# Moving the displaced column blocks of the weights' low parts in the two feed-forward products of a hybrid decoder layer

## The chip, the cores and the metric

One core of a Trainium2 chip runs the kernel alone. The metric is the device time of one execution in microseconds. The kernel before took 2131.19 us, the median of three runs (2129.93, 2131.19 and 2131.62 us).

## The reference

One decoder layer for 512 tokens of width 2048 in fp32, with a hidden width of 8192 in the feed-forward part:

```python
mod = silu(c) @ W_ada + b_ada            # shift1, scale1, gate1, shift2, scale2, gate2
h   = rms_norm(x) * (1 + scale1) + shift1
u   = h @ W_in
# conv group: B * causal_depthwise_conv3(C * H); attention group: NSA, 8 heads
x   = x + gate1 * (concat(rms_norm(y_conv), rms_norm(y_nsa)) @ W_out)
h   = rms_norm(x) * (1 + scale2) + shift2
x   = x + gate2 * (relu(h @ W1) ** 2 @ W2)
out = rms_norm(x)
```

The last product line is what this document is about: `h @ W1` is the first feed-forward product, the product with `W2` is the second.

## The kernel before, in words

**The products.** Each fp32 operand is split in two: a high part, rounded to the reduced format fp32r, and a low part, the rest. A product is then three matmuls on TensorE: high by high, high by low and low by high (`mm3`, line 347). One matmul takes a block of 128 x 128 weights and 256 columns of tokens (half of the 512). In both feed-forward products pairs of rows and columns of blocks are combined by a seven-product scheme: four blobs of weights of 128 x 1024 (`rw`, 512 KB each, loaded by SP's queue) are added and subtracted on VectorE to give seven operands, called B1, U6, T5, B2, T7, B3 and T4 (`operands`, line 1230).

**The weight tiles.** `hilo` (line 1097) makes the two parts of an operand: ScalarE copies the high part into columns of an `hl` tile, and VectorE subtracts it from the source and writes the low part behind it. There are three `hl` tiles (line 1046), used in turn (`hl_tile`, line 1094). A tile has 2048 + 4 * 16 columns of 4 bytes. An operand has eight blocks of 128 columns, and each is used by three matmuls: the high block twice, then the low block. So one tile serves 24 matmuls, and one turn of the ring of three tiles 72. All these matmuls appear in the profile as `pf<-tk,hl` on line 120, since a helper records every instruction there.

**Displacement.** Where the parts stand within a tile is set by the class `Low` (line 1048) and the lists in `rings` (line 1073):

```python
def __getitem__(self, at):                       # L1053
    a, b = at[1].start, at[1].stop
    o = 1024 + self.places[a // P] * SHIFT       # SHIFT = 16 columns = 64 bytes
    return self.t[:, o + a:o + b]
...
def ring(high, *low):                            # L1069
    return cycle([[t[:, high * SHIFT:high * SHIFT + 1024], Low(t, p)] for t, p in zip(hl, low)])
```

`places[k]` says by how many steps of 64 bytes block `k` of the low part stands to the right of column 1024. In stages 1 and 2 the high part itself starts one step in (`high` is 1), so a low block with place 1 is exactly 1024 columns from its high block, and one with place 2 is displaced by 64 bytes against that. `Low.parts` (line 1058) says in how many VectorE instructions the low part is written: one where all places are equal, one with a pattern of 2 x 512 where the only change is at block 4, and otherwise one for each run of equal places.

**The stages.** Stage 0 is the end of the output projection (`w_oa`). Stage 1 (`stage_of[0] = 1`, line 1138) holds the rest of the output projection (`late_out`, line 1151), 24 parts of the first product for p = 0 to 2 (`part`, line 1347), and 29 rounds of `ff1` (line 1277, p = 3 to 31) of seven operands each, whose results go through relu, a square, a split (`outcome`, line 1260) and DRAM. Stage 2 (line 1442) holds the second product, the loop over f, q, seven operands and two halves j at line 1443, where half j = 0 uses blocks 0 to 3 of an operand and j = 1 blocks 4 to 7; then `plain` (line 1421), the last rows as an ordinary product with the final norm (`finish`, line 1394).

**The order.** The instructions from the output projection on are recorded by the class `Order` and put out at line 1493 in an order that it plans itself by its own costs of instructions. A change in the number of VectorE instructions can so move others, on every engine.

Of the kernel before, what the change touches and what calls it, by code (L numbers as in the profile page):

```python
# [273 lines left out]
def hybrid_layer(ctx: ExitStack, tc: tile.TileContext, a, out):  # L274
# [11 lines left out]
    def slot(dtype=F32, name="m"):  # L286
        return mainp.tile([P, SLOT], dtype, name=name, tag="m")
# [90 lines left out]
    ring = [slot(name="wa")[:, :1024] for _ in range(NWA)]  # L378
# [690 lines left out]
    def ring(high, *low):  # L1069
        return cycle([[t[:, high * SHIFT:high * SHIFT + 1024], Low(t, p)] for t, p in zip(hl, low)])  # L1070

    rings = [ring(0, [0] * 8, [0] * 8, [0] * 8), ring(1, [1] * 8, [1] * 8, [1] * 7 + [2]),
             ring(1, [1] * 8, [1] * 8, [1] * 4 + [2] * 4)]
    stage_of = [0]
    ffp.tile([P, SHIFT], F32, name="shift", bufs=1)
    sg = {t: cycle([ffp.tile([P, 1024], d, name="sg", bufs=2) for _ in range(2)])
# [503 lines left out]
```

## Time and profile before

The profiled execution took 2131.37 us, and the span of its trace is 2129.6 us. It stands 0.18 us above the median.

| what | before |
|---|---|
| median of the runs | 2131.19 us |
| the profiled execution, and its span | 2131.37 us, 2129.6 us |
| TensorE (PE) busy | 2071.7 us, 97%, 15014 matmuls |
| VectorE (DVE) busy | 1889.5 us, 89% |
| ScalarE (ACT) busy | 1008.6 us, 47% |
| matmuls `pf<-tk,hl` | 10704, mean 278 ns |
| bytes moved | 454.17 MB, mean 213 GB/s |

A row of groups gives the line, the engine, the operation, what is written and read (output<-inputs, with buffer numbers left out), the shape, the count, the busy time with the mean of one instruction in ns, and the idle time ahead of them with what ended it. A row of the timeline gives start, length in us, engine, line, operation and how many equal instructions in a row it stands for; a bracket at its end is the wait ahead of it, with its releaser. A matmul's duration overlaps the next one's, so TensorE's pace is the distance from start to start: for a row of N matmuls, its length less the duration of one, divided by N - 1.

### The profile page before, as it was taken

The page shows a single profiled execution, that of the slowest core. Times are in us where ns is not written, and L with a number is a line of the kernel's source. Part 1 is how long each engine was busy: PE and PEld are TensorE (multiplying, and loading weights), DVE is VectorE, ACT ScalarE, POOL GpSimd, SP SyncE. Part 2 cuts the span into 40 slices and gives each one's busy share as a digit, 9 for nine tenths or more (in the row PEclk, how much of TensorE's full clock was granted, in tenths as well). Part 3 has the DMA queues.
Part 4 walks back from the last instruction along what each step waited for, and adds up shares of the span by engine and source line. Part 5 has one row for each costly group of instructions (what it writes and reads, how often), then busy time and mean ns, then how long its engine had stood idle before and what let it go on. Part 6 is the DMA issues. An engine that isn't in the chain of part 4 may idle for free.

```text
span 2129.6 us, 38017 instructions
## 1 busy us (share of the span) xinstructions
PE 2071.7 (97%) x15014; PEld 1930.5 (91%) x15014; DVE 1889.5 (89%) x3045; ACT 1008.6 (47%) x1470; POOL 128.6 (6%) x244
## 2 busy tenths in 40 slices
PE   5999999999999999999999999999999999999997
PEld 3888778898877779999999999999999999999997
DVE  8989888887987656999999999999999999999998
ACT  4532333222454434766666666666433333333345
POOL 0000000000000001021221211111000000000000
PEclk8999999999999999999999999999999999999999
DMA  8995679888321144477766677669876366366452
GB/s 333 346 352 221 217 279 326 308 292 314 108 80 40 50 139 158 129 228 208 221 201 202 199 218 215 202 206 306 309 268 230 128 247 236 130 239 237 136 182 90
DMA packets 144130, 454.17 MB, mean 213 GB/s; under 512 B 15824, under 2 KB 20176, under 8 KB 143952
## 3 DMA queue, kind: packets, MB, share of 16 engines
q1 hardware_dynamic: 108816, 386.72, 52.5%
q0 software_dynamic: 34048, 63.98, 9.5%
q8 instruction: 118, 1.93, 0.4%
q10 hardware_dynamic: 1088, 1.05, 0.1%
q14 instruction: 60, 0.49, 0.1%
HBM read 383.53 MB, written 68.16 MB: 212 GB/s over the span
## 4 chain that ended last, share of the span: by engine, by line
PE 55%; DVE 1%; ACT 1%; issue 0%; DMA 0%; DVEq 0%; ACTq 0%
PE pf L120 55%; DVE x L120 0%; DVE hl L120 0%; ACT t L120 0%; ACT x L120 0%; DMA rw<-in_w_f 0%; DVE rw L120 0%; DVE sg L120 0%; DVE sacc L120 0%; ACT hl L120 0%; DVE t L120 0%; ACT tk L120 0%; DVE gt L120 0%; DVEq L1576 0%; ACT sacc L120 0%
## 5 line engine op out<-in xcount | busy, mean ns | idle before, releaser
L120 PE MATMUL pf<-tk,hl 128*128 128x256 f32 x10704 | 1235.5, 278 | 2.3 <-ACT t L120 1.4
L120 PEld LDWEIGHTS pf<-tk,hl 128*128 128x128 f32 x10704 | 1233.6, 188 | 3.1 <-ACT t L120 1.6
L120 ACT ACTIVATE hl<-rw 128x1024 fp32r<-128x1024 f32 x269 | 285.4, 1062 | 337.5 <-PE pf L120 302.7
L120 DVE TENSOR_TENSOR hl<-rw,hl 128x1024 fp32r<-128x1024 f32 (+2 forms) x314 | 331.9, 1064 | 36.5 <-ACT hl L120 36.5
L120 ACT ACTIVATE hl<-sg 128x1024 fp32r<-128x1024 f32 x180 | 191.1, 1062 | 230.1 <-PE pf L120 203.5
L120 PE MATMUL ps<-h_m,wh 128*128 128x512 f32 x1080 | 252.6, 390 | 0.0
L120 DVE SCALAR_TENSOR_TENSOR t<-wa,cs 128x1024 bf16<-128x1024 f32 x192 | 234.2, 1220 | 20.0 <-DMA wa<-in_w_ada 18.0
L120 PEld LDWEIGHTS ps<-h_m,wh 128*128 128x128 f32 x1080 | 201.6, 188 | 41.5
L120 ACT ACTIVATE wh<-raw 128x1024 fp32r<-128x1024 f32 (+1 forms) x106 | 112.7, 1063 | 251.8 <-PE ps L120 204.1
L120 DVE TENSOR_TENSOR hl<-sg,hl 128x1024 fp32r<-128x1024 f32 (+2 forms) x170 | 185.6, 1101 | 31.8 <-ACT hl L120 31.1
L120 PE MATMUL ps<-h,wh 128*128 128x512 f32 x840 | 200.7, 395 | 5.7 <-ACT h L120 3.3
L120 PEld LDWEIGHTS ps<-h,wh 128*128 128x128 f32 x840 | 159.1, 191 | 41.6 <-ACT h L120 5.3
L120 DVE TENSOR_TENSOR wh<-raw,wh 128x1024 fp32r<-128x1024 f32 (+1 forms) x106 | 129.9, 1226 | 24.3 <-ACT wh L120 23.5
L120 DVE SCALAR_TENSOR_TENSOR x<-pf,mod,x 128x256 f32<-128x256 f32 (+1 forms) x280 | 133.6, 486 | 17.7 <-PE pf L120 16.7
L120 DVE TENSOR_TENSOR sg<-sg,rw 128x1024 f32<-128x1024 f32 x120 | 146.0, 1217 | 0.1
L120 POOL DMA_DIRECT2D g<-gt x192 | 101.5, 533 | 408.6 <-ACT hl L120 237.7
L120 PE MATMUL pw<-mix,wh 128*128 128x512 f32 x384 | 109.8, 406 | 0.0
L120 ACT ACTIVATE t<-t 128x512 f32<-128x512 f32 (+3 forms) x131 | 74.7, 571 | 16.3 <-DVE t L120 14.3
L120 PEld LDWEIGHTS pw<-mix,wh 128*128 128x128 f32 x384 | 69.7, 190 | 11.0 <-issue 0.5
L120 DVE TENSOR_TENSOR sg<-rw 128x1024 f32<-128x1024 f32 x60 | 73.0, 1217 | 7.2 <-DMA rw<-in_w_f 4.8
L120 DVE TENSOR_TENSOR rw<-rw 128x1024 f32<-128x1024 f32 x60 | 72.9, 1216 | 0.0
L120 DVE TENSOR_TENSOR gt<-t,gt 128x512 fp32r<-128x512 f32 x96 | 65.5, 683 | 2.0 <-PE pf L120 1.1
(204 smaller groups left out, 1782.4 us busy)
## 6 DMA issues: line engine op xcount, KB each, us to landing
rw<-in_w_f SPq DMA_DIRECT2D x263, 512.0 KB, 3.9
wa<-in_w_ada SPq DMA_DIRECT2D x192, 512.0 KB, 6.0
tk<-g SPq DMA_DIRECT2D x114, 512.0 KB, 5.9
g<-gt POOLq DMA_DIRECT2D x192, 256.0 KB, 4.6
raw<-in_w_conv SPq DMA_DIRECT2D x32, 512.0 KB, 5.0
x<-in_xt SPq DMA_DIRECT2D x16, 512.0 KB, 5.3
raw<-in_w_kv SPq DMA_DIRECT2D x16, 512.0 KB, 4.6
raw<-in_w_cv SPq DMA_DIRECT2D x16, 512.0 KB, 3.8
```

What stands on the lines that cost most here:

```text
L120: x.i, x.eng, x.call = len(self.nodes), eng, (lambda: real(*args, **kw))
```

## The change

Only the lists of places change. In stage 1 no block is displaced any more (before: block 7 in the third tile). In stage 2 the second tile gets its block 7 displaced, and the third tile has its blocks 6 and 7 displaced where it had 4 to 7.

```diff
-    rings = [ring(0, [0] * 8, [0] * 8, [0] * 8), ring(1, [1] * 8, [1] * 8, [1] * 7 + [2]),
-             ring(1, [1] * 8, [1] * 8, [1] * 4 + [2] * 4)]
+    rings = [ring(0, [0] * 8, [0] * 8, [0] * 8), ring(1, [1] * 8, [1] * 8, [1] * 8),
+             ring(1, [1] * 8, [1] * 7 + [2], [1] * 6 + [2] * 2)]
```

The matmuls stay the same in number, size and, but for two places where a few small ones of a norm move, in order. By `Low.parts` the number of VectorE instructions changes: in stage 1 the third tile's low part is one instruction where it was two (896 and 128 columns); in stage 2 the second tile's is two (896 and 128) where it was one, and the third tile's is two (768 and 256) where it was one of 2 x 512.

VectorE in the middle of the second product, before. `hl_5694`, `hl_5695` and `hl_5696` are the first, second and third tile, `rw` blobs of weights, `sg` sums of blobs, `pf` results of TensorE, `x1` the residual stream:

```order
L120 TENSOR_TENSOR hl_5696<-rw_5693,hl_5696 128x2x512
L120 SCALAR_TENSOR_TENSOR x1_5885<-pf_5714,mod_106,x1_5885 128x256
L120 SCALAR_TENSOR_TENSOR x1_5886<-pf_5715,mod_106,x1_5886 128x256
L120 TENSOR_TENSOR hl_5694<-rw_5689,hl_5694 128x1024
L120 SCALAR_TENSOR_TENSOR x1_5885<-pf_5716,mod_106,x1_5885 128x256
L120 SCALAR_TENSOR_TENSOR x1_5886<-pf_5717,mod_106,x1_5886 128x256
L120 TENSOR_TENSOR hl_5695<-sg_5701,hl_5695 128x1024
L120 SCALAR_TENSOR_TENSOR x1_5885<-pf_5714,mod_106,x1_5885 128x256
L120 TENSOR_TENSOR sg_5701<-sg_5701,rw_5692 128x1024
L120 SCALAR_TENSOR_TENSOR x1_5886<-pf_5715,mod_106,x1_5886 128x256
L120 TENSOR_TENSOR hl_5696<-sg_5700,hl_5696 128x2x512
```

VectorE at the same place of the changed kernel:

```order
L120 TENSOR_TENSOR hl_5694<-rw_5689,hl_5694 128x1024
L120 SCALAR_TENSOR_TENSOR x1_5885<-pf_5716,mod_106,x1_5885 128x256
L120 SCALAR_TENSOR_TENSOR x1_5886<-pf_5717,mod_106,x1_5886 128x256
L120 TENSOR_TENSOR hl_5695<-sg_5701,hl_5695 128x896
L120 SCALAR_TENSOR_TENSOR x1_5885<-pf_5714,mod_106,x1_5885 128x256
L120 TENSOR_TENSOR hl_5695<-sg_5701,hl_5695 128x128
L120 TENSOR_TENSOR sg_5701<-sg_5701,rw_5692 128x1024
L120 TENSOR_TENSOR hl_5696<-sg_5700,hl_5696 128x768
L120 SCALAR_TENSOR_TENSOR x1_5886<-pf_5715,mod_106,x1_5886 128x256
L120 TENSOR_TENSOR hl_5696<-sg_5700,hl_5696 128x256
```

Each split low part is two instructions now, and the updates of the residual stream stand between the two pieces instead of between whole low parts.

ScalarE shortly before part 16 of the first product, before. `t<-pf` takes the relu of half a result out of its bank, `t_84<-pf_5714` that of a bank into which TensorE goes on summing from part 16 on; `t<-t` squares, `tk` and `gt` are high parts of tokens and of results, `hl<-rw` high parts of weights:

```order
L120 ACTIVATE t_80<-pf_5718 128x256
L120 ACTIVATE tk_5874<-t_81 128x2x256
L120 ACTIVATE hl_5694<-rw_5692 128x1024
L120 ACTIVATE t_80<-t_80 128x512
L120 ACTIVATE t_84<-pf_5713 128x256
L120 ACTIVATE gt_5705<-t_80 128x2x256
L120 ACTIVATE t_84<-pf_5714 128x256
L120 ACTIVATE hl_5695<-rw_5693 128x1024
```

ScalarE at the same place of the changed kernel:

```order
L120 ACTIVATE t_80<-pf_5718 128x256
L120 ACTIVATE tk_5874<-t_81 128x2x256
L120 ACTIVATE t_80<-t_80 128x512
L120 ACTIVATE hl_5694<-rw_5692 128x1024
L120 ACTIVATE t_84<-pf_5713 128x256
L120 ACTIVATE gt_5705<-t_80 128x2x256
L120 ACTIVATE tk_5876<-t_83 128x2x256
L120 ACTIVATE t_84<-pf_5714 128x256
L120 ACTIVATE hl_5695<-rw_5693 128x1024
```

One copy of tokens (`tk_5876`) has moved ahead of `t_84<-pf_5714`, and the high part of a weight tile behind `t_80<-t_80`. The order of the matmuls around it is the same.

## The prediction

> **What bounds the kernel now.** I read the page first: its busy times, its slices and its chain of waits.
>
> ```profile
> span 2129.6 us, 38017 instructions
> PE 2071.7 (97%) x15014; PEld 1930.5 (91%) x15014; DVE 1889.5 (89%) x3045; ACT 1008.6 (47%) x1470; POOL 128.6 (6%) x244
> PE 55%; DVE 1%; ACT 1%; issue 0%; DMA 0%; DVEq 0%; ACTq 0%
> ```
>
> PE is busy 97% of the span and carries nearly the whole chain; DVE comes next with 89%. Next I split the feed-forward part into stretches: first product, start of the second, second product, end.
>
> ```profile
> core 0: us, PE busy (x) PEld busy (x) DVE busy (x) ACT busy (x) POOL busy (x), PEclk, DMA share, GB/s
> 930.00:1483.00 553.00, 553.00 (x4870) 553.00 (x4869) 523.98 (x767) 355.41 (x495) 107.47 (x204) 1.00 0.70 214
> 1483.00:1545.00 62.00, 61.09 (x521) 60.61 (x520) 55.47 (x77) 28.08 (x35) 4.13 (x8) 1.00 0.87 320
> 1545.00:2090.00 545.00, 545.00 (x4672) 545.00 (x4672) 514.18 (x717) 215.26 (x218) 1.14 (x3) 1.00 0.57 199
> 2090.00:2129.60 39.60, 27.38 (x228) 26.28 (x226) 29.20 (x66) 19.79 (x50) 0.00 (x0) 0.87 0.30 107
> ```
>
> In the first and third stretch PE never stops, and the clock is 1.00. Yet a matmul takes 553.00 / 4870 = 113.55 ns in the one and 545.00 / 4672 = 116.65 ns in the other, though all have 256 columns. So something other than waits and clock sets the pace. Grouping the matmuls of short windows shows two kinds (the first row from the second product at 1625 us, the other from the first product at 1129 us), and the timeline their pace:
>
> ```profile
> L120 PE MATMUL pf<-tk,hl 128*128 128x256 f32 x61 | 7.3, 281 | 0.0
> L120 PE MATMUL pf<-tk,hl 128*128 128x256 f32 x66 | 7.6, 276 | 0.0
> 1129.14 7.64 PE L120 MATMUL pf<-tk,hl 128*128 128x256 f32 x66
> 1624.82 7.11 PE L120 MATMUL pf<-tk,hl 128*128 128x256 f32 x59
> 1642.83 5.83 PE L120 MATMUL pf<-tk,hl 128*128 128x256 f32 x50
> ```
>
> The pace is (7.64 - 0.276) / 65 = 113.29 ns in the first product and (7.11 - 0.281) / 58 = 117.74 ns in this stretch of the second; 18 us later it is (5.83 - 0.276) / 49 = 113.35 ns. I call these the short and the long pace: 4.45 ns apart, or 0.32 us in a turn of the ring of 72 matmuls. Read matmul by matmul, the second product has one turn at the short pace, then two at the long, again and again, and the step between them falls each time on the third tile, the one with four displaced blocks. The kernel is bound by PE's pace, and PE keeps to one pace until displaced blocks move it to the other.
>
> **How the pace moves.** Rows in which no block is displaced, the first two from the output projection, the others from the end of the second product:
>
> ```profile
> 845.87 2.99 PE L120 MATMUL pf<-mixa,sg 128*128 128x256 f32 x24
> 848.69 2.99 PE L120 MATMUL pf<-mixa,gt 128*128 128x256 f32 x24
> 2092.79 2.75 PE L120 MATMUL pf<-tk,hl 128*128 128x256 f32 x22
> 2103.62 1.98 PE L120 MATMUL pf<-tk,hl 128*128 128x256 f32 x16
> ```
>
> These run at 117.8, 117.8, 117.6 and, the last, 113.6 ns. So either pace is kept while nothing is displaced, also from the third tile over to the first. Two rows show what displaced blocks do:
>
> ```profile
> 1129.14 8.68 PE L120 MATMUL pf<-tk,hl 128*128 128x256 f32 x75
> 1641.08 1.46 PE L120 MATMUL pf<-tk,hl 128*128 128x256 f32 x11
> ```
>
> The first covers a whole turn in the first product with its one displaced block: 8.68 - 0.276 - 74 x 0.11329 = 0.02 us over the short pace, and short again behind it. The second begins near the last two of the four displaced blocks of a third tile entered long, and ends short: 1.46 - 0.276 - 10 x 0.11329 = 0.05 us over. In a third tile that is entered short, the first two displaced blocks begin with the same pattern of paces, and the other two leave it long. So I read: from the short pace, one displaced block leads back to short for 0.02 us, two lead back to short for 0.05 us, four lead to long.
>
> **The change, part by part.** The sum is made against the profiled execution of 2131.37 us, 0.18 above the median.
>
> *First product, nothing displaced.* If PE enters it short, it stays short, and the small excess goes: 553.00 - 4870 x 0.11329 = 1.3 us. **-1.3** (rivals below for a long entry). Its entry is the last place where PE stops:
>
> ```profile
> 904.58 3.34 PE L120 MATMUL pf<-tk,hl 128*128 128x256 f32 x27 [1.44 <-ACT t L120]
> 907.82 1.42 PE L120 MATMUL pf<-tk,sg 128*128 128x256 f32 x10
> 905.12 1.06 ACT L120 ACTIVATE hl<-rw 128x1024 fp32r<-128x1024 f32 x1
> 906.09 0.62 ACT L120 ACTIVATE t<-t 128x512 f32<-128x512 f32 x1
> 906.61 0.36 ACT L120 ACTIVATE t<-pf 128x256 f32<-128x256 f32 x1
> 906.87 0.62 ACT L120 ACTIVATE gt<-t 128x512 fp32r<-128x512 f32 x1
> 907.39 0.37 ACT L120 ACTIVATE t<-pf 128x256 f32<-128x256 f32 x1
> 913.38 186.83 PE L120 MATMUL pf<-tk,hl 128*128 128x256 f32 x1643
> ```
>
> Part 16 begins at 907.82, just after ACT's last step ends at 907.76; the last row, of the first product right behind, has (186.83 - 0.276) / 1642 = 113.61 ns, short but for the displaced blocks. ACT's new order puts a copy of tokens into this chain and takes `t<-t` out in front of it. The copy has the shape of `gt<-t`, 0.52 us to the next start, as long as the 0.52 us of `t<-t`. So I expect the stop of about 0.17 us to stay, and the entry at the short pace with it.
>
> *Second product.* Its turn has one displaced block in the second tile and two in the third. From short that is 72 x 0.11329 + 0.02 + 0.05 = 8.23 us, against 545.00 / (4672 / 72 = 64.9 turns) = 8.40 us. **-11.1**. The excess of two blocks is taken from an entry at the long pace; between 0.02 and 0.10 us it moves this term by -2 to +3. A long entry into the product would mend itself if one block does from long what it does from short, which no row shows.
>
> *Start of the second product.* Its 521 matmuls at 113.29 ns would be 59.0 us of 62.00, so 3.0 us are long pace and waits:
>
> ```profile
> 1532.26 13.98 PE L120 MATMUL pf<-tk,hl 128*128 128x256 f32 x116 [0.86 <-DVE hl L120]
> 1499.32 1.22 DVE L120 TENSOR_TENSOR sg<-rw 128x1024 f32<-128x1024 f32 x1 [2.12 <-DMA rw<-in_w_f]
> ```
>
> DVE waits for weights here (0.87 of the DMA time is taken) and PE for DVE, so a faster pace mostly waits longer. I take **-0.5**, between 0 and -1.5.
>
> *End.* PE is busy in 27.38 of the last 39.60 us, and waits for the norm's steps:
>
> ```profile
> 2117.54 0.61 PE L120 MATMUL pf<-ones,sacc 128*128 128x1 f32 x4 [1.48 <-DVE sacc L120]
> 2119.25 0.86 PE L120 MATMUL pf<-t,ones 128*128 128x256 f32 x2 [1.10 <-DVE t L120]
> ```
>
> There a DVE with more pieces is late by itself: three or four splits are 0.2 us. I take **+0.5**, between -1 (226 matmuls from long to short) and +2 (the two waits nearly doubled).
>
> *The pieces on DVE.* Two pieces in the first product, then whole instructions:
>
> ```profile
> 1130.49 1.28 DVE L120 TENSOR_TENSOR hl<-sg,hl 128x896 fp32r<-128x896 f32 x2
> 1131.69 0.68 DVE L120 TENSOR_TENSOR gt<-t,gt 128x512 fp32r<-128x512 f32 x1
> 1132.29 1.22 DVE L120 TENSOR_TENSOR sg<-sg,rw 128x1024 f32<-128x1024 f32 x1
> 1133.43 1.21 DVE L120 TENSOR_TENSOR hl<-rw,hl 128x1024 fp32r<-128x1024 f32 x1
> ```
>
> Start to start two pieces take 1.20 us and one whole 1.14 us, so a split costs 0.06. The first product loses one per turn, which DVE did not need: zero. The second gains two, 64.9 x 0.12 = 7.8 us. DVE idles there for 545.00 - 514.18 = 30.8 us, and its idle time ahead of the low parts comes from ACT, which waits for free tiles, so from PE:
>
> ```profile
> L120 DVE TENSOR_TENSOR hl<-rw,hl 128x1024 fp32r<-128x1024 f32 x112 | 136.4, 1218 | 10.4 <-ACT hl L120 10.4
> L120 DVE TENSOR_TENSOR hl<-sg,hl 128x1024 fp32r<-128x1024 f32 x84 | 102.5, 1221 | 14.7 <-ACT hl L120 14.0
> ```
>
> After the change DVE has 522.0 us of work in 533.9. That is cover, and thin: 11.9 us, 2%. I take zero; if the cover goes, half the gain goes with it (a rival).
>
> Sum: -1.3 - 11.1 - 0.5 + 0.5 = **-12.4**, so 2131.37 - 12.4 = 2119.0 for an execution like the profiled one, 2118.8 for the median. This case's own range is 2116 to 2123.
>
> **The rivals.** *The first product runs at the long pace throughout (slower).* In the kernel before, the one displaced block could mend a long pace each turn; now nothing in 29 rounds does. If the stop ahead of part 16 is only partial, or the tokens copied earlier let PE start without it, PE may pass 907.8 us at the long pace, as 845.87 and 848.69 show it kept. Then 4870 matmuls take 117.74 ns: 573.4 for 553.00, +20.4, and about 196 ahead of 930 us add 0.9; with the other terms (-11.1, 0) 2131.2 + 10.2 = about 2141. For it: ACT's order changes just there. Against: the equal sum above. Chance 0.11.
>
> *DVE becomes the bound of the second product.* With 98% of its time taken, low parts come late and PE waits. Half of 11.1 us lost gives about 2124. For it: 2% cover. Against: DVE is at 523.98 / 553.00 = 95% in the first product, and PE never waits. Chance 0.09.
>
> *The new places don't hold the short pace.* If two displaced blocks leave PE at the long pace, the first tile and most of the second, some 46 matmuls, are long in each turn: 0.2 us, 64.9 times 13 us, which takes the gain. About 2130. The same comes out where the pace does not hang on places at all, but on something that merely coincides with the third tile. Chance 0.07. The Trainium skill speaks for this one: "TensorE: Matmul & The Clock Gate", in "Step-by-step: what each phase is for", gives PE two independent SBUF read ports, so that the load of the next weights takes no read bandwidth from the running matmul. By that rule the place of a weight block could not matter, and the time would stay about 2130; the trace speaks against it with 116.65 ns in the second product, where four blocks are displaced, and 113.55 in the first, where one is.
>
> **How the numbers follow.** The forecast has the rest, 0.73, and its time is 2118.8. The range from 2115 to 2127 holds it, with a microsecond below for terms that fall the same way, and the case of late DVE; about 2 in 10 are left out. A measurement of this kernel can tell about 0.2%, 4.3 us, from no change, so 2126.9 and 2135.5 are the bounds: faster 0.73 + 0.09 = 0.82, same 0.07, slower 0.11.
>
> **What would show it.** In the changed profile: a mean pace of 113.3 ns from 930 us to the end of the first product, with no excess; about 114.3 ns in the second (8.23 / 72), and no row of 281 ns that lasts longer than a few matmuls; DVE idle about 12 us in the steady part of the second product, still behind ACT; a full stop of PE before part 16. It is wrong if a stretch of 117.7 ns fills the first product, if PE's rows in the second name DVE as releaser many times, or if turns at 117.7 ns come back behind the third tile.

## The result, and the profile after

The changed kernel took 2141.47 us, the median of four runs (2139.89 to 2144.40), against 2130.56 us for the kernel before (four runs, 2129.75 to 2131.62). The ratio is 1.0053, with a 95% interval of 1.0035 to 1.0070: slower by half a per cent, where 2118.8 was forecast.

The page of the changed kernel, the rows that answer to the first three shown of before:

```profile
span 2137.8 us, 38103 instructions
PE 2080.2 (97%) x15014; PEld 1938.8 (91%) x15014; DVE 1894.6 (89%) x3118; ACT 1009.8 (47%) x1470; POOL 128.6 (6%) x244
PE 79%; DVE 6%; DMA 2%; ACT 1%; issue 1%; DVEq 0%; SPq 0%; ACTq 0%
```

PE is busy for 8.5 us more with the same 15014 matmuls, so the time was not lost to waits alone. To compare stage with stage the stretches must hold the same work, not the same microseconds. The next two fences divide both traces at the same matmuls: parts 0 to 23, the 29 rounds of the first product, the first 520 matmuls of the second, its steady rest, the last stage up to its last feed-forward matmul, and a first piece behind it. The first is the kernel before.

```profile
core 0: us, PE busy (x) PEld busy (x) DVE busy (x) ACT busy (x) POOL busy (x), PEclk, DMA share, GB/s
860.98:929.74 68.76, 67.24 (x585) 66.70 (x583) 63.10 (x120) 49.45 (x88) 8.36 (x16) 1.00 0.54 164
929.74:1483.26 553.52, 553.52 (x4875) 553.52 (x4873) 524.50 (x767) 355.58 (x495) 107.73 (x204) 1.00 0.70 215
1483.26:1545.40 62.14, 61.23 (x523) 60.75 (x521) 55.61 (x78) 28.34 (x36) 4.54 (x9) 1.00 0.87 320
1545.40:2092.56 547.16, 547.16 (x4691) 547.16 (x4690) 516.34 (x721) 217.29 (x222) 0.74 (x2) 1.00 0.57 198
2092.56:2115.78 23.22, 23.07 (x199) 22.82 (x198) 19.91 (x48) 15.94 (x41) 0.00 (x0) 1.00 0.24 84
2115.78:2119.54 3.76, 1.17 (x8) 0.90 (x7) 1.83 (x5) 1.19 (x3) 0.00 (x0) 1.00 0.14 48
```

And the changed kernel:

```profile
core 0: us, PE busy (x) PEld busy (x) DVE busy (x) ACT busy (x) POOL busy (x), PEclk, DMA share, GB/s
857.62:927.17 69.55, 69.08 (x584) 68.73 (x583) 63.54 (x115) 49.29 (x88) 9.19 (x17) 1.00 0.53 169
927.17:1500.99 573.82, 573.82 (x4875) 573.82 (x4873) 522.86 (x702) 355.70 (x495) 106.90 (x202) 1.00 0.66 207
1500.99:1562.38 61.39, 60.20 (x522) 59.71 (x521) 56.10 (x91) 28.43 (x36) 4.60 (x9) 1.00 0.88 316
1562.38:2098.52 536.14, 535.93 (x4690) 535.72 (x4689) 519.55 (x847) 215.47 (x215) 0.68 (x2) 1.00 0.58 202
2098.52:2123.67 25.15, 23.17 (x199) 22.84 (x198) 22.71 (x55) 18.30 (x49) 0.00 (x0) 1.00 0.21 73
2123.67:2127.70 4.03, 1.44 (x9) 1.10 (x7) 1.83 (x5) 1.40 (x4) 0.00 (x0) 0.83 0.21 72
```

The second column is the length of each stretch. The first product takes 20.3 us longer, though PE is busy in all of it, at full clock, with the same matmuls. The steady second product takes 11.0 us less. The rest is small: parts +0.8, start of the second product -0.8, last stage +1.9, its tail +0.3. Ahead of the parts the changed kernel is 3.4 us earlier (857.62 for 860.98); the kernels below begin their parts anywhere from 855.65 to 861.92, also where their code up to there is the same as before, so this is scatter between executions. The sum is +8.1, and the spans differ by 8.2.

The pace shows why. A group of matmuls from the middle of the first product of the changed kernel, and timeline rows from its first and its second product:

```profile
L120 PE MATMUL pf<-tk,hl 128*128 128x256 f32 x64 | 7.7, 281 | 0.0
927.76 200.50 PE L120 MATMUL pf<-tk,hl 128*128 128x256 f32 x1701
1599.81 40.46 PE L120 MATMUL pf<-tk,hl 128*128 128x256 f32 x353
```

In the first product a matmul is 281 ns long and follows the last one after (200.50 - 0.281) / 1700 = 117.8 ns: the long pace, without a break for all 29 rounds. In the second it is (40.46 - 0.276) / 352 = 114.2 ns, as forecast (114.3). Where it became long for good is seen at the two stops of PE around part 15:

```profile
900.65 3.91 PE L120 MATMUL pf<-tk,hl 128*128 128x256 f32 x32 [0.47 <-ACT t L120]
904.46 3.09 PE L120 MATMUL pf<-tk,sg 128*128 128x256 f32 x24
907.39 2.87 PE L120 MATMUL pf<-tk,gt 128*128 128x256 f32 x23
```

Read matmul by matmul, PE runs at 118 ns up to the first stop and at 113 ns between the two; around the start of part 16, at 904.46, there are two distances of 173 and 222 ns; and from there on it is 118 ns: the third row has (2.87 - 0.281) / 22 = 117.7. In the kernel before, the two distances at the same place are 171 and 222 ns, and four matmuls later the pace is 113. The stop is the same within 2 ns, and PE leaves it at the other pace.

### The profile page after: what moved, and what is told of

It is laid out like the page before. It is cut to its first block, busy times and chain, and to the rows that moved or that the text cites. A ratio compares the mean times of both kernels' runs of the same rounds, so it can differ in the third digit from the quotient of the medians.

```text
span 2137.8 us, 38103 instructions
## 1 busy us (share of the span) xinstructions
PE 2080.2 (97%) x15014; PEld 1938.8 (91%) x15014; DVE 1894.6 (89%) x3118; ACT 1009.8 (47%) x1470; POOL 128.6 (6%) x244
## 4 chain that ended last, share of the span: by engine, by line
PE 79%; DVE 6%; DMA 2%; ACT 1%; issue 1%; DVEq 0%; SPq 0%; ACTq 0%
PE pf L120 61%; PE ps L120 12%; PE pw L120 3%; PE pv L120 1%; PE s L120 1%; PE pt L120 1%; DVE nm L120 1%; DMA raw<-in_cmp_w 1%; DVE x L120 1%; DVE hl L120 1%; DMA raw<-in_w_conv 1%; DVE wh L120 1%; DMA rw<-in_w_f 1%; DVE p L120 0%; DVE tt L120 0%
## 5 line engine op out<-in xcount | busy, mean ns | idle before, releaser
L120 DVE TENSOR_TENSOR hl<-rw,hl 128x1024 fp32r<-128x1024 f32 (+4 forms) x355 | 337.1, 959 | 42.0 <-ACT hl L120 41.1
L120 DVE TENSOR_TENSOR hl<-sg,hl 128x1024 fp32r<-128x1024 f32 (+4 forms) x212 | 190.4, 911 | 29.8 <-ACT hl L120 29.7
L120 PEld LDWEIGHTS pw<-mix,wh 128*128 128x128 f32 x384 | 69.6, 190 | 10.9 <-issue 0.5
```

What stands on the lines that cost most here:

```text
L120: x.i, x.eng, x.call = len(self.nodes), eng, (lambda: real(*args, **kw))
```

## The experiments

Theory A: PE keeps its pace until displaced blocks, or a stop, move it; with nothing displaced, whatever pace the last stop leaves is kept for the whole first product. Theory B: a stage without displaced blocks is long by itself. Theory C: not the places but the number and order of VectorE's and ScalarE's instructions make the pace. Where places are given, they replace the lists of the changed kernel's `rings`, or those of the experiment that the text names. Ratios are against the kernel before, which was run beside each experiment with medians of 2129.26 to 2130.49 us.

**1. Stage 2 of the change alone.**

```diff
-    ring(1, [1] * 8, [1] * 8, [1] * 8),
+    ring(1, [1] * 8, [1] * 8, [1] * 7 + [2]),
```

> Stage 1 as before (block 7 of the third tile displaced), stage 2 as in the changed kernel. Theory A (PE keeps a pace until displaced blocks or a stop move it; the loss of the changed kernel is the first product held at the long pace): the second product's 11 us are kept and the first product runs short, near 113.6 ns a matmul; about 2121 us against about 2131 of the kernel before. Theory B (without a displaced block the pace is long by itself, whatever the entry) and theory C (the number and order of VectorE's and ScalarE's instructions set the pace, not the places): also about 2121. If the second product's gain was not real it comes out at 2131.

It took 2123.09 us (nine runs), ratio 0.9965 (0.9953 to 0.9977). First product and steady second product:

```profile
924.36:1477.87 553.51, 553.51 (x4874) 553.51 (x4873) 524.52 (x769) 355.83 (x495) 107.33 (x203) 1.00 0.69 214
1541.41:2077.08 535.67, 535.67 (x4690) 535.67 (x4689) 519.57 (x846) 215.48 (x215) 0.53 (x2) 1.00 0.58 203
```

The first product is back at 553.5 and the second keeps its gain, 547.16 to 535.67. The whole is 2 us above the expectation; the last stage took 26.75 us here for 23.22, at a granted clock of 0.94 (more on this in experiment 6).

**2. Stage 1 of the change alone.**

```diff
-    ring(1, [1] * 8, [1] * 7 + [2], [1] * 6 + [2] * 2)]
+    ring(1, [1] * 8, [1] * 8, [1] * 4 + [2] * 4)]
```

> Stage 1 as in the changed kernel (nothing displaced), stage 2 as before. Theory A: long in the first product if its last stop ends as in the changed kernel, then 2131 + 20.3 - 3 = about 2148; if that stop ends short, about 2127. Theory B and C: about 2148.

It took 2151.74 us (five runs), ratio 1.0103 (1.0090 to 1.0117).

```profile
931.22:1505.04 573.82, 573.82 (x4875) 573.82 (x4873) 522.77 (x700) 355.71 (x495) 106.90 (x202) 1.00 0.66 207
1567.83:2114.80 546.97, 546.97 (x4691) 546.97 (x4689) 516.30 (x721) 217.31 (x222) 0.74 (x2) 1.00 0.56 198
```

The first product is long as in the changed kernel, the second is as before. By these stages the two halves of the change add up, one worth +20 us and the other -11. The whole times do less well: they are 22.0 us above and 6.7 us below (experiment 1) the kernel before, and both halves together 10.9 above. Nor did the 2148 us that were expected come out: 3 us were taken off there for the earlier start of the changed kernel's parts, which this kernel does not have (861.67 us, for 860.98 before and 857.62 changed).

**3. Displaced only ahead of the 29 rounds.** The lists of the first experiment, and a third stage without displaced blocks for the rounds:

```diff
+    ring(1, [1] * 8, [1] * 8, [1] * 8)]      # a ring 3
...
+    stage_of[0] = 3
     for p in range(NP, 32):
         ff1(p)
```

> As the first kernel of this call, but the block is displaced only up to part 23; the 29 rounds of the first product have nothing displaced. Theory A: they are entered short and stay short for 4870 matmuls with no excess, 113.29 ns each; about 2120, 1.3 below the first kernel. Theory B: 117.74 ns in the 29 rounds, 2121 + 20.4 = about 2141. Theory C (whole low parts on VectorE in the rounds, as in the changed kernel): about 2141.

It took 2121.29 us (six runs), ratio 0.9955 (0.9941 to 0.9969).

```profile
930.69:1482.85 552.16, 552.16 (x4875) 552.16 (x4873) 520.81 (x702) 355.74 (x495) 107.41 (x203) 1.00 0.69 215
```

The first product has the short pace throughout with nothing displaced: 29 x 7 x 24 = 4872 matmuls in 552.16 us are 113.33 ns each, 1.36 us less than with one displaced block per turn. Theory B falls, and theory C with it as far as it rested on whole low parts in the rounds: those of this kernel are as whole as those of the changed one (702 VectorE instructions in both).

**4. Split, but not displaced.** Every instruction and its order as in experiment 1, against which the edit is shown; only the address of block 7 is that of the undisplaced place.

```diff
-    cut = [k for k in range(1, 8) if self.places[k] != self.places[k - 1]]
+    cut = [k for k in range(1, 8) if self.places[k] != self.places[k - 1]] or self.cut
...
-    ring(1, [1] * 8, [1] * 8, [1] * 7 + [2]),
+    cut_ring([(), (), (7,)]),                # all places 1, third tile written in two pieces
```

> As the first kernel of this call in every instruction and its order, the third tile's low part still written in pieces of 896 and 128 columns, but with nothing displaced in stage 1. Theory A: one pace from the last stop ahead of part 16 to the end of the first product, long (about 2141) or short (about 2120), nothing between. Theory B: about 2141. Theory C: as the first kernel, about 2121.

Its twelve runs fall into two groups with nothing between: seven from 2117.13 to 2125.18 us and five from 2140.20 to 2144.06. (Their common median of 2124.40 and the ratio of 0.9994, 0.9965 to 1.0022, describe neither.) The profiled execution, 2142.07 us, is one of the five:

```profile
927.99:1501.81 573.82, 573.82 (x4875) 573.82 (x4873) 526.34 (x769) 354.14 (x495) 106.56 (x202) 1.00 0.67 207
```

One program, and in some executions it is 20 us longer than in others. That is what theory A says and neither rival does. Only one of the executions has a trace, so that the lower group ran short in the first product is read from its times. (Experiments 5 and 6 show both ways out in traces.) The two ways are not equally likely everywhere: the changed kernel (four runs) and experiment 2 (five), which have nothing displaced in stage 1 either, were long every time. What tips them is open.

**5. One displaced block per turn in both stages.**

```diff
+    ring(1, [1] * 8, [1] * 8, [1] * 7 + [2]),    # stage 1
+    ring(1, [1] * 8, [1] * 8, [1] * 7 + [2])]    # stage 2
```

> In both stages only block 7 of the third tile is displaced, so one mended step of 0.02 us in each turn and one split of a low part instead of two in the second product. Theory A: the steady part of the second product at 72 x 0.11329 + 0.02 = 8.18 us a turn, 5 us less than with three displaced blocks, less PE time lost to VectorE at the end; about 2117, some 13 below the kernel before. Rival (the second product needs more displaced blocks than the first to be held short, since its halves of 4 blocks come in another order): it stays at 2129 or above.

It took 2117.89 us (five runs), ratio 0.9950 (0.9937 to 0.9962).

```profile
925.75:1479.27 553.52, 553.52 (x4874) 553.52 (x4873) 524.44 (x768) 355.50 (x495) 107.16 (x204) 1.00 0.69 214
1541.75:2074.72 532.97, 532.97 (x4690) 532.80 (x4689) 514.64 (x782) 215.31 (x216) 0.75 (x2) 1.00 0.58 203
```

The steady second product is 2.7 us shorter than with three displaced blocks. The 5 us expected were badly worked out: 0.05 us less in each of 65 turns is 3.3. The whole is below both kernels of the comparison.

**6. The same without displaced blocks in the last stage.**

```diff
+    stage_of[0] = 3                          # a ring with all places 1
     plain(3)
```

> As the first kernel of this call, with nothing displaced in the last stage, so no splits there. If the extra 2 to 4 us of the last stage in the changed kernel come from VectorE's split low parts, they go: 1 to 2 us below the first kernel. If they come from where the norm's matmuls stand in PE's order, or the stage is entered long, no gain, or 0.8 us more (191 matmuls x 4.45 ns).

It took 2118.91 us (five runs), ratio 0.9951 (0.9937 to 0.9964), no better than experiment 5. Its last stage:

```profile
2076.61:2103.88 27.27, 24.98 (x200) 24.41 (x198) 22.59 (x53) 18.22 (x47) 0.00 (x0) 0.94 0.22 77
```

It is not shorter without the splits (25.35 us in experiment 5), but the granted clock is 0.94 here and 1.00 there. So here are both stages in two parts each, up to the end of PE's wait for the sum of squares (`pf<-ones,sacc`) and behind it; the first two rows are of experiment 6, the others of experiment 5:

```profile
2076.61:2092.14 15.53, 13.25 (x115) 12.85 (x113) 15.06 (x38) 14.87 (x39) 0.00 (x0) 1.00 0.00 1
2092.14:2103.88 11.74, 11.74 (x85) 11.56 (x85) 7.53 (x15) 3.35 (x9) 0.00 (x0) 0.85 0.51 178
2074.72:2090.19 15.47, 13.68 (x115) 13.28 (x114) 15.14 (x39) 15.03 (x39) 0.00 (x0) 1.00 0.01 1
2090.19:2100.07 9.88, 9.88 (x85) 9.83 (x85) 7.43 (x15) 3.29 (x9) 0.00 (x0) 1.00 0.56 195
```

Up to the wait the two are as long as each other, 15.53 and 15.47 us at full clock; the difference lies behind it, at a granted clock of 0.85 for 1.00. So the splits are not what makes the end longer.

The two experiments show one thing more. Up to the last stage their instructions on PE, VectorE and ScalarE are the same, in the same order. The 24 matmuls `pf<-tk,gt` shortly behind the stop at part 16, in experiment 5 and in experiment 6:

```profile
906.67 2.88 PE L120 MATMUL pf<-tk,gt 128*128 128x256 f32 x24
907.95 2.99 PE L120 MATMUL pf<-tk,gt 128*128 128x256 f32 x24
```

They run at (2.88 - 0.276) / 23 = 113.2 ns and at (2.99 - 0.281) / 23 = 117.8 ns: the same instructions leave the stops at either pace. In experiment 6 the next displaced block, at about 913.4 us, leads back to short (distances of 122, 120, 116 and 114 ns, then 113), so its first product takes the same 553.52 us.

**7. Five splits instead of one.** Places as in experiment 5, against which the edit is shown; low parts of the first two tiles are written in three pieces in stage 2.

```diff
-    ring(1, [1] * 8, [1] * 8, [1] * 7 + [2])]
+    cut_ring([(2, 5), (2, 5), ()], [1] * 8, [1] * 8, [1] * 7 + [2])]
```

> As the first kernel of this call in its places, but the low parts of the first and second tile are written in three pieces each in the second product (256, 384 and 384 columns), five splits per turn instead of one. At 0.06 us a split VectorE has 7.92 + 0.3 = 8.22 us of work in a turn of 8.18, so if VectorE is next behind PE, PE waits for low parts and the time rises by 3 to 8 us. If VectorE's cover is larger than read, no change.

It took 2116.91 us (five runs), ratio 0.9942 (0.9930 to 0.9955): no loss.

```profile
1540.19:2073.21 533.02, 533.02 (x4690) 532.93 (x4689) 527.52 (x1039) 215.42 (x214) 2.10 (x4) 1.00 0.58 204
```

VectorE is busy for 527.52 of 533.02 us, 99%, and PE never waits. The four extra splits cost it 527.52 - 514.64 = 12.9 us in 65 turns, 0.05 us each, and they only eat its idle time. The expectation that it would become the bound was wrong.

**8. to 10. How many blocks, together or apart.** These took the third tile's displaced blocks through other numbers.

```diff
+    three (5 to 7) in stage 1, all eight in stage 2:        [1] * 5 + [2] * 3    and  [2] * 8
+    five (3 to 7) in stage 1, seven (1 to 7) in stage 2:    [1] * 3 + [2] * 5    and  [1] + [2] * 7
+    six (2 to 7) in stage 1, blocks 1, 4, 7 in stage 2:     [1] * 2 + [2] * 6    and  [1, 2, 1, 1, 2, 1, 1, 2]
```

> Stage 1: three displaced blocks in the third tile (5 to 7). Stage 2: the whole low part of the third tile displaced, all eight blocks, nothing in the others. One look at the paces. Theory A with a count of displaced blocks: one and two lead back to the short pace and four to the long, so three either leads back (113.6 to 114 ns in the first product) or leaves the long pace for part of the turns (115 to 117 ns); eight is twice four, two steps on, so a mix in the second product. If only the change of place between neighbouring blocks within a tile mattered, eight equal places would act like none, and the second product would keep its pace of entry throughout.

> Stage 1: five displaced blocks in the third tile (3 to 7). Stage 2: seven (1 to 7). One look. The runs so far fit a count that goes on with each displaced block and closes at five: a turn that ends with 0, 1 or 2 over leads back to the short pace when nothing is displaced, one that ends with 3 or 4 over stays long (3: short and long turns in alternation; 4: one short, two long; 8: alternation). By this count five and seven, though more than three and four, hold the short pace: near 114 ns in both products (553 to 557 us for the first; the second 11 to 13 us under that of the kernel before in its steady part). Rival (the more displaced blocks, the more long turns): 116 ns or more in both.

> Stage 1: six displaced blocks in the third tile (2 to 7). Stage 2: three displaced, but apart from each other (blocks 1, 4 and 7 of the third tile). One look. By the count that closes at five, six acts like one: near 114 ns in the first product. The three apart each lead back to short before the next comes, so the second product is short, near 114 ns with about three times the excess of one (0.06 us a turn). Rival (a count of displaced blocks per turn alone decides): three apart act like three together, alternation, about 116 ns.

The whole times were 2142.53, 2128.19 and 2124.38 us, one run each. First product and steady second product, of three and eight:

```profile
929.77:1494.52 564.75, 564.75 (x4875) 564.75 (x4873) 525.70 (x767) 355.21 (x495) 106.66 (x203) 1.00 0.68 210
1557.14:2103.13 545.99, 545.99 (x4691) 545.99 (x4690) 515.53 (x720) 217.28 (x222) 0.58 (x2) 1.00 0.56 198
```

of five and seven:

```profile
929.40:1486.55 557.15, 557.15 (x4874) 557.15 (x4873) 525.23 (x768) 355.61 (x495) 107.10 (x204) 1.00 0.69 213
1548.56:2087.70 539.14, 539.14 (x4691) 539.14 (x4689) 515.38 (x783) 216.35 (x218) 0.74 (x2) 1.00 0.57 201
```

and of six and three apart:

```profile
928.05:1486.55 558.50, 558.50 (x4874) 558.50 (x4873) 525.88 (x772) 355.66 (x495) 107.24 (x204) 1.00 0.68 213
1545.91:2081.36 535.45, 535.45 (x4691) 535.45 (x4689) 526.70 (x1038) 214.74 (x214) 1.10 (x3) 1.00 0.58 202
```

Three and eight alternate: one turn of the ring short, one long, which the timeline of three in the first product shows (a long stretch, then a short one):

```profile
1040.74 8.88 PE L120 MATMUL pf<-tk,hl 128*128 128x256 f32 x74
1049.22 5.85 PE L120 MATMUL pf<-tk,hl 128*128 128x256 f32 x50
```

Here are (8.88 - 0.281) / 73 = 117.8 ns and (5.85 - 0.276) / 49 = 113.8 ns, the latter with its first steps behind the displaced blocks. Five, six and seven hold the short pace between their displaced blocks: 557.15 and 558.50 us over 4872 matmuls are 114.4 and 114.6 ns, and 539.14 us over 4690 (seven) are 115.0, although more is displaced than with three. Three apart are short as well, with (535.45 - 4690 x 0.11329) / 65 = 0.06 us over the short pace in a turn. The rivals "more is longer" and "the number in a turn alone" fall. Of the expected sizes, that of five was missed narrowly (557.15 for 553 to 557 us) and that of seven clearly: 8.0 us under the 547.16 of before instead of 11 to 13, since each turn pays for seven blocks on the way.

**11. All displaced; and one by 128 bytes.**

```diff
+    ring(1, [2] * 8, [2] * 8, [2] * 8),          # stage 1
+    ring(1, [1] * 8, [1] * 8, [1] * 7 + [3])]    # stage 2
```

> Stage 1: all low blocks of all three tiles displaced by 64 bytes. Stage 2: block 7 of the third tile displaced by 128 bytes. One look. If a displaced block acts by its distance from its high block (1024 columns and 64 bytes instead of 1024 columns), the pace never settles in the first product: a longer matmul once in five blocks, a mean near 118 ns. If it acts only as a change of place from one low block to the next, equal places act like none, and the first product keeps one pace, 113.3 or 117.7 ns. For 128 bytes in the second product: like two displaced blocks if the step counts by its bytes (about 0.05 us a turn, short), like one if it counts as one (0.02 us).

One run of 2137.86 us. First product and steady second product:

```profile
925.59:1501.57 575.98, 575.98 (x4874) 575.98 (x4873) 524.43 (x701) 355.78 (x495) 106.54 (x202) 1.00 0.66 206
1563.49:2095.01 531.52, 531.52 (x4690) 531.50 (x4689) 514.66 (x782) 215.60 (x216) 0.74 (x2) 1.00 0.58 204
```

With all low blocks alike the pace never settles: 575.98 / 4872 = 118.2 ns. Distances from start to start in ns, read from the trace, of 24 matmuls (eight blocks) of the first product:

```
119 120 118 116 118 114 124 120 115 120 118 117 118 121 116 119 120 117 116 118 115 123 120 116
```

The mark 114 or 115, then 124 or 123, comes back after 15 matmuls, which is five blocks. So a low block acts by where it stands, most simply by its distance from its high block, and not by a change from one low block to the next. (The high parts stand at the same place of the tile in all these runs, so distance and place were not told apart.) The block displaced by 128 bytes does neither of the things expected: the second product has 531.52 / 4690 = 113.33 ns, no excess at all, as if nothing were displaced.

**12. The changed kernel, with displaced blocks in one round.** The closest kernel to the changed one: only the round p = 3 has block 7 of the third tile displaced, three tiles in all.

```diff
     for p in range(NP, 32):
+        stage_of[0] = 3 if p == NP else 1        # ring 3: [1] * 8, [1] * 8, [1] * 7 + [2]
         ff1(p)
```

> The changed kernel with block 7 of the third tile displaced in the first of the 29 rounds only (p = 3, two or three tiles); the stops of PE ahead of part 16 and the 28 rounds behind stay as in the changed kernel. Theory A (a kept pace, a count that closes at five, so one or two displaced blocks lead from long to short): long up to the round p = 3, then short with nothing displaced to the end of the first product; about 19 us below the changed kernel, near 2121. If the long pace came from the 29 rounds themselves (whole low parts, their order, the tiles), two or three displaced blocks in the first round change nothing: about 2141.

It took 2120.40 us (twelve runs), ratio 0.9962 (0.9945 to 0.9978). The timeline of its profiled execution behind the stop, and from the round p = 4 on:

```profile
902.96 3.09 PE L120 MATMUL pf<-tk,sg 128*128 128x256 f32 x24
905.89 2.99 PE L120 MATMUL pf<-tk,gt 128*128 128x256 f32 x24
908.72 18.54 PE L120 MATMUL pf<-tk,hl 128*128 128x256 f32 x156
950.09 200.08 PE L120 MATMUL pf<-tk,hl 128*128 128x256 f32 x1764
```

Parts 16 to 23 are long, as in the changed kernel: (18.54 - 0.281) / 155 = 117.8 ns. The first displaced block comes at about 928.3 us, and the pace behind it is short; from 950 us on it is (200.08 - 0.276) / 1763 = 113.3 ns with nothing displaced. Three displaced blocks are worth 21.1 us (2141.47 to 2120.40; the first product alone takes 552.31 us for 573.82). Eleven of the runs lie between 2116.76 and 2121.01; one took 2137.71 us. That one has no trace, and what happened in it stays open.

## Why the prediction was wrong

The forecast failed at one step, the entry of the first product: "So I expect the stop of about 0.17 us to stay, and the entry at the short pace with it." The first half held: the distances at the stop are 173 and 222 ns for 171 and 222. The second half does not follow from it. I had read from the stop of one trace that it lets PE start short. Experiments 4 to 6 show that PE may start either way, from one execution to the next of the same instructions. The trace of the kernel before held the warning too: two breaks of PE at matmuls of a norm, whose first distances behind them are 305 and 306 ns, are left at different paces.

```profile
840.26 5.77 PE L120 MATMUL pf<-mixa,hl 128*128 128x256 f32 x46
867.79 2.97 PE L120 MATMUL pf<-tk,hl 128*128 128x256 f32 x23
```

Without these first distances the rows run at (5.77 - 0.305 - 0.281) / 44 = 117.8 ns and (2.97 - 0.306 - 0.276) / 21 = 113.7 ns.

What made the kernel before safe was not its entry but its one displaced block per turn, at a price of 0.02 us a turn, 1.36 us in all (experiment 3). In experiments 6 and 12 the first displaced block leads back from long to short. It need not be the first: in the kernel before, the displaced block just ahead of 845.87 us is passed at the long pace (distances of 121 and 116 ns) and PE stays long behind it, as the prediction's own row of 117.8 ns there shows. The change gave up this repair to save 1.36 us, and its first product took 20.3 us longer.

The result is the first rival with its place, price and point of decision: it gave +20.4 us for the rounds, +0.9 ahead of them and about 2141 in all; measured were +20.3, +0.8 and 2141.47. That the whole agrees so closely is partly luck: the rival put the start of the second product and the end at nothing together, where the profiled executions have -0.8 and +2.2, and scatter ahead of the parts moves a time by some microseconds (the spans of the two profiled executions are 8.2 us apart, the medians 10.9). Its chance of 0.11 was too low. The stop's exit should have been treated as unknown, since the prediction had one stop of one execution at that place, with three distances of 116 to 120 ns behind it before the pace was short.

Point by point, the rest by its terms:
- *First product, nothing displaced: -1.3.* Right as a term for a short entry (-1.36 in experiment 3), and worth +20.3 at a long one.
- *Second product: -11.1.* Measured -11.0 in the changed kernel, -11.5 in experiment 1. That one block leads from long to short, which no row had shown, is seen at the start of the second product of the changed kernel, which is entered long and is short from its first displaced block on; that a single block does not always do this is said above.
- *Start of the second product: -0.5.* Measured -0.8.
- *End: +0.5, up to +2.* Measured +1.9 in the last stage and +0.3 behind it, a little over the upper end. The reason given was wrong: it is not the splits (experiment 6). PE waits there for the sum of squares, in the changed kernel

```profile
2113.99 0.60 PE L120 MATMUL pf<-ones,sacc 128*128 128x1 f32 x4 [1.98 <-DVE sacc L120]
```

  and the chain ahead of this wait goes through ScalarE's and VectorE's steps of the norm. From the start of the stage to this row it takes 15.47 us for 13.19 before, and 15.47 and 15.53 in experiments 5 and 6. The stage is longer in all kernels with a shorter second product, so some of the gain is given back there; whether by the earlier arrival of PE or by the other order was not taken apart. Part of the length is the clock, not the work: these stages take 24.6 to 25.5 us where the granted clock is 1.00, 26.5 to 27.3 where it is 0.94 (experiments 1, 3 and 4 among them), and 28.3 at 0.88 (experiment 12), for 23.2 to 23.5 at 1.00 in the others.
- *The pieces on VectorE: 0.06 us each and hidden.* They cost 0.05 and are hidden, even five in a turn (experiment 7). The rival of a late VectorE falls.
- *The rival that the places do not matter.* It falls with experiments 4 and 11. The Trainium skill, in "TensorE: Matmul & The Clock Gate", "Step-by-step: what each phase is for", says that the load of the next weights takes no read bandwidth from the running matmul. The runs differ from what the forecast took this rule to mean: low blocks 64 bytes further away change the pace from 113.3 to 118.2 ns at the same instructions. Whether reading is what they disturb, no run here shows.

What is shown, then: the pace is kept where nothing is displaced (experiments 3, 4 and 12); displaced blocks move it; with one, two, five, six or seven in a tile and turn it comes back to short, with three, four or eight it goes round through long turns, and displaced without end it shows a cycle of five blocks. A count that closes at five fits all of these: over it, 0, 1 or 2 settle short, and 3 or 4 settle long, so that from long one block can lead to short (from 4) or stay long (from 3), and both are seen. It was formed after three and eight had been seen, and five, six, seven and the three apart were forecast by it. What in the chip counts so is not shown.

## What to carry to other kernels

Where PE is never idle, look at the distance from start to start of its matmuls, and group them by duration: two paces 4% apart can hide in one mean, at full clock. If a pace can be kept for hundreds of microseconds, ask of a change not only what it costs per turn but what repairs a bad entry; a cheap repair in each turn is worth more than a forecast of the entry, which two executions of one program need not share. And a spread of times in two groups, as in experiment 4, is a finding: a median over it means nothing.

## What was not expected of the hardware

- A low block that stands 64 bytes off the even distance of 4096 bytes from its high block disturbs the pace, and one that stands 128 bytes off does not (118.2 ns with all blocks at 64 bytes, 113.33 ns with one in 24 at 128).
- The cycle of five blocks, 15 matmuls, with all blocks at 64 bytes.
- Two stops of equal length within 2 ns (171 and 173, then 222) are left at 113.3 and at 117.7 ns, and the same instructions leave one place at 113.2 and at 117.8 ns in two executions (experiments 5 and 6).
- The two paces are not all there are: in the kernel before, 53 matmuls `pf<-mixa,kw` from 851.52 us on take 6.52 us, (6.52 - 0.28) / 52 = 120.0 ns each. Their high and low parts lie in two tiles of their own.
- VectorE can be busy for 99% of 533 us (527.52) without PE waiting for it once.
